# The 24 adaptive sums of layer 0's attention as products on GpSimd and accumulating copies on ScalarE

## The chip, the cores and the metric

One core of a Trainium2 chip runs the whole program. The metric is the device time of one execution in microseconds. The names in the rows are those of the profile: PE is TensorE, PEld its weight loads, DVE is VectorE, ACT is ScalarE, POOL is GpSimd, SP is the engine that issues nearly all transfers.

## What is computed

A two-layer encoder on 512 positions of width 1024. In each layer a vector `c` gives six modulation vectors, three kinds of attention run side by side on groups of heads (differential, dilated windows, two-dimensional neighbourhood), and a gated MLP with a short convolution follows.

```
for l in range(DEPTH):
    mod = jax.nn.silu(c) @ w_ada[l] + b_ada[l]
    sh_a, sc_a, gt_a, sh_f, sc_f, gt_f = [m[:, None, :] for m in jnp.split(mod, 6, axis=-1)]
    h = rms_norm(x, g_attn[l]) * (1.0 + sc_a) + sh_a
    x = x + gt_a * hybrid_mixer(h, w_in[l], ...)
    h = rms_norm(x, g_ffn[l]) * (1.0 + sc_f) + sh_f
    x = x + gt_f * conv_glu_ffn(h, w_up[l], ...)
return rms_norm(x, g_final)
```

The change concerns `mod`: 6144 numbers a layer, each a sum of 1024 products and a bias.

## The kernel before

The activations stand transposed, 128 features on the partitions by 512 positions. Every large product is made on PE as three float32r products (`mm3`, L493 to L495: high times high, high times low, low times high). So each block of weights is loaded as float32 into a buffer of the pool tag `raw` (four buffers; `emit_raw`, L333), ACT casts it to its high part (`whi`, `fhi`, L355), and the rest `raw - whi` is written as the low part in pieces of 256 columns by POOL (L361) or in one piece by DVE (L363), by the kind of weight.

The modulation isn't made on PE. `ada_list` names 96 blocks of 128 outputs, 48 for a layer. For each, `ada_load` (L400 to L410) brings 128 columns of `w_ada` (transposed, 128x1024, 512 KB) into a buffer: the first 16 into buffers of their own, all later ones into the same four `raw` buffers that the weights go through. `ada_step` (L412 to L432) then lets DVE multiply the block with `silu(c)` (`cb`), sum it up along the row and add the bias in one instruction (L422; a second, short one reads the accumulator), which gives one column of `mod`. For the two scale vectors ACT makes `gsc`, `(1 + mod) * g`, from it (L430). Then `ada_step` issues the next load at once, so one block is under way at a time.

The sums run inside other work. `attention_phase` has a list of units (projections, scores, softmax, outputs) and a `Clock`: `ck.after(lag, f)` runs `f` so many ticks later in program order. In layer 0, from the tenth unit on, every fourth tick calls `ada_step` until 40 blocks are done; what is left is done in a loop at the end of the phase (L1216). These are blocks 16 to 39: the gate of the attention, and shift and scale of the FFN. The FFN of layer 0 makes the remaining 56, one every four of its ticks. There are no sums in layer 1.

`ffn_phase` first finishes the output projection (`o2`, four weight units). Each result is added to `x` on DVE (L1223), squared on ACT (L452) and the squares are added up on POOL (L454), first for columns 0 to 255 of all eight blocks, then for the others. PE sums the first half over the partitions (`Norm.stats`, L463), DVE and POOL make the root (L466, L468), and the normed input `h` goes into the gate products (`g0`, `u0`). Order on PE: the first half of `o2`, two blocks of the second half, the statistics of the first half, the rest of the second half, then the gate.

A scheduler orders instructions on each engine, each engine's queue runs in order, and a pool's buffer goes to the next load that asks after it was freed.

Of the kernel before, what the change touches and what calls it, by code (L numbers as in the profile page):

```python
# [14 lines left out]
BF16 = mybir.dt.bfloat16  # L15
AF = mybir.ActivationFunctionType
ALU = mybir.AluOpType
# [4 lines left out]
D = 1024  # L22
# [144 lines left out]
OFF_B = 0  # L167
OFF_GA = OFF_B + NB_ADA
OFF_GF = OFF_GA + DEPTH * 8
# [7 lines left out]
def build(ctx, tc, a):  # L177
    nc = tc.nc
    V, A, G, PE, SY = nc.vector, nc.scalar, nc.gpsimd, nc.tensor, nc.sync
# [14 lines left out]
    def uid():  # L194
        cnt[0] += 1
        return cnt[0]
# [5 lines left out]
    def tmp(shape=(128, 512), dt=F32, tag="tmp", bufs=TMP_BUFS):  # L202
        return wp.tile(list(shape), dt, tag=tag, bufs=bufs, name=f"{tag}{uid()}")

    par = cp.tile([128, NPAR], F32, name="par")
    cb = cp.tile([128, D], F32, name="cb")
# [20 lines left out]
    mod = [cp.tile([128, 48], F32, name=f"mod{l}") for l in range(DEPTH)]  # L227
    gsc = [cp.tile([128, 16], F32, name=f"gsc{l}") for l in range(DEPTH)]
# [83 lines left out]
    ck = Clock()  # L312
# [85 lines left out]
    ada_st = {"n": 0}  # L398

    def ada_load():  # L400
        i = ada_st["n"] + len(ada_raw)
        if i >= len(ada_list):
            return
        l, j = ada_list[i]
        if i < 16:
            r = fpool["p"].tile([128, D], F32, tag="araw", bufs=10, name=f"araw{uid()}")
        else:
            r = wp.tile([128, D], F32, tag="raw", bufs=4, name=f"raw{uid()}")
        SY.dma_start(r, a["w_ada"][l, j])
        ada_raw.append(r)  # L410

    def ada_step():  # L412
        if ada_st["n"] >= len(ada_list):
            return
        if not ada_raw:
            ada_load()
        l, j = ada_list[ada_st["n"]]
        cv = cx if ada_st["n"] < 16 else cb
        r = ada_raw.pop(0)
        ada_st["n"] += 1  # L420
        junk = tmp((128, D), BF16)
        V.tensor_tensor_reduce(out=junk, in0=r, in1=cv, op0=ALU.mult, op1=ALU.add, scale=1.0,  # L422
                               scalar=par[:, OFF_B + l * 48 + j:OFF_B + l * 48 + j + 1],
                               accum_out=mod[l][:, j:j + 1])
        g, k = divmod(j, 8)
        if g in (1, 4):
            o = 0 if g == 1 else 8
            base = OFF_GA if g == 1 else OFF_GF
            g = par[:, base + l * 8 + k:base + l * 8 + k + 1]
            A.activation(out=gsc[l][:, o + k:o + k + 1], in_=mod[l][:, j:j + 1], func=AF.Identity, scale=g, bias=g)  # L430
        if ada_st["n"] >= 16 or ada_st["n"] + len(ada_raw) < 16 and l == 0:
            ada_load()  # L432
# [74 lines left out]
    def first_g0():  # L507
# [47 lines left out]
        with tc.issue_after(last.ins):  # L555
            ada_step()
        ada_step()
        norm_x(0)
        norm_x(1)
        mk(0)  # L560
        norm_x(2)
        norm_x(3)
        ada_step()
        ada_step()
        mk(1)
# [827 lines left out]
    out = a["out"].rearrange("m p n -> p m n")  # L1393
# [62 lines left out]
```

## Time and profile before

| what | value |
|---|---|
| median of 3 runs | 1336.28 us (1334.36 to 1337.09) |
| the profiled execution | 1336.97 us, its span 1335.1 us (1.9 us lie around the span) |
| granted clock of PE, mean | 0.988 |
| busy PE / PEld | 1283.9 / 1100.8 us (96% / 82%) |
| busy DVE | 843.5 us (63%) |
| busy ACT | 632.0 us (47%) |
| busy POOL | 276.3 us (21%) |
| 80 sums on DVE (L422) | 106.9 us, 1336 ns each; idle before them 65.1 us |

The span goes from the first to the last instruction on record. In layer 0 the attention with its projections takes from about 56 to 295 us: differential scores to 143.9 us, the dilated part to 228.8, the neighbourhood part to 295, then the last projection and the norm ahead of the FFN, which begins to multiply at about 319 us. An engine's idle time is put down to what released it.

### The profile page before, as it was taken

What the parts mean: (1) busy time and instruction counts of PE and PEld (TensorE: products, weight loads), DVE (VectorE), ACT (ScalarE), POOL (GpSimd) and SP (SyncE); (2) the same over time, 40 slices, a digit from 0 to 9 for tenths busy, and PEclk for the clock granted to TensorE, in tenths of its full rate; (3) what the DMA queues carried; (4) which work ended last, traced back from release to release, by engine and by line L of the source; (5) the groups of instructions that cost most, each with busy time, mean ns of one, the idle gap of its engine ahead of it and who ended that gap; (6) DMA issues with size and microseconds to landing.
All of it is one profiled execution on the core that took longest, in us unless ns stands there. A gap on an engine that the chain in (4) does not pass through costs nothing.

```text
span 1335.1 us, 18663 instructions
## 1 busy us (share of the span) xinstructions
PE 1283.9 (96%) x6836; PEld 1100.8 (82%) x6836; DVE 843.5 (63%) x1538; ACT 632.0 (47%) x1138; POOL 276.3 (21%) x351
## 2 busy tenths in 40 slices
PE   6989899889999999999999999999999999999997
PEld 5878688779988888888899878988898888888886
DVE  6669777688776566656766596566775434443443
ACT  5446588665533233323342577887553313331331
POOL 4646623243000000000022465323500000000002
PEclk9999999899999999999999999999999999999999
DMA  9776568853465656665523856572343333333211
GB/s 360 253 205 179 173 201 215 237 158 126 147 206 181 203 171 190 193 201 166 175 81 116 205 144 193 145 205 83 115 127 95 95 97 97 95 96 103 77 36 63
DMA packets 75003, 207.30 MB, mean 155 GB/s; under 512 B 8608, under 2 KB 12576, under 8 KB 74784
## 3 DMA queue, kind: packets, MB, share of 16 engines
q1 hardware_dynamic: 74048, 203.72, 50.9%
q10 hardware_dynamic: 864, 2.39, 0.5%
q8 instruction: 54, 0.88, 0.3%
q14 instruction: 37, 0.30, 0.1%
HBM read 180.91 MB, written 15.73 MB: 147 GB/s over the span
## 4 chain that ended last, share of the span: by engine, by line
PE 77%; DMA 10%; DVE 5%; POOL 3%; issue 3%; ACT 2%; SPq 1%; POOLq 0%; DVEq 0%; ACTq 0%
PE pr L495 10%; PE pr L493 10%; PE pr L494 10%; PE s L494 5%; PE s L493 5%; PE s L495 5%; PE pt L494 4%; PE pt L493 4%; PE pt L495 4%; DMA raw<-w 3%; PE pt L923 2%; PE o L494 2%; PE o L495 2%; PE o L493 2%; DMA raw<-w_ada 2%
## 5 line engine op out<-in xcount | busy, mean ns | idle before, releaser
L355 ACT CAST whi<-raw 128x1024 fp32r<-128x1024 f32 (+2 forms) x136 | 128.3, 944 | 240.0 <-PE pr L495 76.9
L454 POOL TENSOR_TENSOR tmp<-tmp,tmp 128x256 f32<-128x256 f32 (+1 forms) x38 | 38.6, 1017 | 708.2 <-ACT tmp L452 707.2
L361 POOL TENSOR_TENSOR wlo<-raw,whi 128x256 fp32r<-128x256 f32 (+1 forms) x170 | 123.8, 759 | 226.0 <-ACT whi L355 201.7
L363 DVE TENSOR_TENSOR wlo<-raw,whi 128x1024 fp32r<-128x1024 f32 (+1 forms) x86 | 100.3, 1167 | 101.8 <-ACT whi L355 101.1
L422 DVE CUSTOM_DVE_ANT_0 tmp<-raw,cb,par 128x1024 bf16<-128x1024 f32 x80 | 106.9, 1336 | 65.1 <-DMA raw<-w_ada 64.8
L355 ACT CAST fhi<-raw 128x1024 fp32r<-128x1024 f32 (+1 forms) x76 | 74.5, 985 | 129.3 <-PE pr L495 51.8
L363 DVE TENSOR_TENSOR flo<-raw,fhi 128x1024 fp32r<-128x1024 f32 (+1 forms) x74 | 86.5, 1169 | 55.5 <-ACT fhi L355 54.7
L493 PE MATMUL pr<-h,whi 128*128 128x512 f32 (+1 forms) x300 | 112.8, 376 | 1.4 <-DVE tmp L677 0.7
L495 PE MATMUL pr<-h,whi 128*128 128x512 f32 (+1 forms) x300 | 111.9, 373 | 0.4 <-DVE h L489 0.4
L494 PE MATMUL pr<-h,wlo 128*128 128x512 f32 (+1 forms) x300 | 112.1, 374 | 0.0
L493 PE MATMUL pr<-h,fhi 128*128 128x512 f32 (+1 forms) x244 | 86.9, 358 | 0.1
L494 PE MATMUL pr<-h,flo 128*128 128x512 f32 (+1 forms) x244 | 86.7, 357 | 0.0
L495 PE MATMUL pr<-h,fhi 128*128 128x512 f32 (+1 forms) x244 | 85.9, 358 | 0.3 <-DVE h L489 0.3
L1281 ACT ACTIVATE tmp<-tmp 128x512 f32<-128x512 f32 x44 | 27.6, 631 | 80.1 <-DVE tmp L1276 80.1
L493 PEld LDWEIGHTS pr<-h,whi 128*128 128x128 f32 x300 | 56.9, 190 | 10.3 <-ACT whi L355 1.0
L495 PEld LDWEIGHTS pr<-h,whi 128*128 128x128 f32 x300 | 56.9, 190 | 9.5 <-DVE h L489 0.6
L494 PEld LDWEIGHTS pr<-h,wlo 128*128 128x128 f32 x300 | 57.0, 190 | 8.5
L931 DVE TENSOR_TENSOR pl<-pt,ph 128x512 fp32r<-128x512 f32 x80 | 54.5, 684 | 14.0 <-ACT ph L927 13.8
L927 ACT CAST ph<-pt 128x512 fp32r<-128x512 f32 x80 | 46.5, 583 | 29.1 <-PE pt L923 28.4
L1017 DVE TENSOR_REDUCE sm<-s 128x1 f32<-128x512 f32 x64 | 43.0, 681 | 21.1 <-PE s L1015 20.7
L1025 ACT ACTIVATE tmp<-s,sm 128x512 f32<-128x512 f32 x64 | 43.8, 690 | 18.9 <-DVE sm L1017 16.5
L493 PE MATMUL pr<-oh,whi 128*128 128x512 f32 (+1 forms) x128 | 49.7, 388 | 3.0 <-ACT oh L1164 3.0
(288 smaller groups left out, 3694.6 us busy)
## 6 DMA issues: line engine op xcount, KB each, us to landing
raw<-w SPq DMA_DIRECT2D x132, 512.0 KB
raw<-w_ada SPq DMA_DIRECT2D x80, 512.0 KB
raw<-w SPq DMA_DIRECT2D x64, 384.0 KB
araw<-w_ada SPq DMA_DIRECT2D x16, 512.0 KB
raw<-w SPq DMA_DIRECT2D x16, 320.0 KB
graw<-w SPq DMA_DIRECT2D x8, 384.0 KB
scr0b<-nat SPq DMA_DIRECT2D x12, 256.0 KB
qs<-nat SPq DMA_DIRECT2D x24, 128.0 KB
```

Of the source, the lines that this page charges most:

```text
L355: A.copy(hi, r)
L361: G.tensor_tensor(out=lo[:, c:e], in0=r[:, c:e], in1=hf[:, c:e], op=ALU.subtract)
L363: V.tensor_tensor(out=lo, in0=r, in1=hi.bitcast(F32), op=ALU.subtract)
L422: V.tensor_tensor_reduce(out=junk, in0=r, in1=cv, op0=ALU.mult, op1=ALU.add, scale=1.0, scalar=par[:, OFF_B + l * 48 + j:OFF_B + l * 48 + ...
L454: self.last = self.eng.tensor_tensor(out=self.sq[0][:, sl], in0=self.sq[0][:, sl], in1=self.sq[m][:, sl], op=ALU.add)
L493: PE.matmul(out, wh, hh, start=first, stop=False)
L494: PE.matmul(out, wl, hh, start=False, stop=False)
L495: return PE.matmul(out, wh, hl, start=False, stop=last)
L927: A.copy(st["ph", half][:, :, sl], pt)
L931: V.tensor_tensor(out=st["pl", half][:, :, sl], in0=st["pt", qb], in1=st["ph", half][:, :, sl].bitcast(F32), op=ALU.subtract)
L1017: V.tensor_reduce(out=nm[:, m:m + 1], in_=s, axis=AX.X, op=ALU.max, negate=True)
L1025: A.activation(out=Ps[m], in_=ss[m], func=AF.Exp, bias=nm[:, m:m + 1], accum_out=dn if m else ld)
```

## The change

For blocks 16 to 39 of layer 0 the instruction on DVE is gone. In its place POOL multiplies the block with `cb` in four pieces of 256 columns, in place in the `raw` buffer. Two ticks later ACT copies the product as bf16 into a scratch tile and accumulates along the row, adds the bias with a second instruction, and makes `gsc` where needed. The load of the next block is issued only there, behind ACT's copy, no longer at once. The 16 blocks ahead and the 56 blocks behind stay as they are. Lines behind L420 have numbers higher by 21.

```diff
--- before.py
+++ after.py
@@ -418,6 +418,27 @@
         cv = cx if ada_st["n"] < 16 else cb
         r = ada_raw.pop(0)
         ada_st["n"] += 1
+        g, k = divmod(j, 8)
+        if l == 0 and 16 <= ada_st["n"] - 1 < 40:
+            for c0 in range(0, D, 256):
+                G.tensor_tensor(out=r[:, c0:c0 + 256], in0=r[:, c0:c0 + 256], in1=cb[:, c0:c0 + 256], op=ALU.mult)
+
+            def fin():
+                junk = tmp((128, D), BF16)
+                acc = tmp((128, 1), tag="sm1", bufs=12)
+                b = par[:, OFF_B + l * 48 + j:OFF_B + l * 48 + j + 1]
+                A.activation(out=junk, in_=r, func=AF.Copy, accum_out=acc)
+                A.activation(out=mod[l][:, j:j + 1], in_=acc, func=AF.Identity, bias=b)
+                if g in (1, 4):
+                    o = 0 if g == 1 else 8
+                    base = OFF_GA if g == 1 else OFF_GF
+                    gp = par[:, base + l * 8 + k:base + l * 8 + k + 1]
+                    A.activation(out=gsc[l][:, o + k:o + k + 1], in_=mod[l][:, j:j + 1], func=AF.Identity,
+                                 scale=gp, bias=gp)
+                ada_load()
+
+            ck.after(2, fin)
+            return
         junk = tmp((128, D), BF16)
         V.tensor_tensor_reduce(out=junk, in0=r, in1=cv, op0=ALU.mult, op1=ALU.add, scale=1.0,
                                scalar=par[:, OFF_B + l * 48 + j:OFF_B + l * 48 + j + 1],
```

The order on POOL in the dilated part, before. `wlo` are the low parts of weights, `sm` a root.

```order
L986 TENSOR_TENSOR sm_1815<-sm_1812,mh 128x8
L361 TENSOR_TENSOR wlo_1878<-raw_1663,whi_1877 128x256 x3
L361 TENSOR_TENSOR wlo_2002<-raw_1774,whi_2001 128x256 x3
L361 TENSOR_TENSOR wlo_2113<-raw_1883,whi_2112 128x256 x3
L361 TENSOR_TENSOR wlo_2205<-raw_2007,whi_2204 128x256 x4
```

The same place after:

```order
L361 TENSOR_TENSOR wlo_1908<-raw_1681,whi_1907 128x256 x3
L424 TENSOR_TENSOR raw_1929<-raw_1929,cb 128x256 x4
L361 TENSOR_TENSOR wlo_2038<-raw_1798,whi_2037 128x256 x3
L424 TENSOR_TENSOR raw_2064<-raw_2064,cb 128x256 x4
L361 TENSOR_TENSOR wlo_2155<-raw_1913,whi_2154 128x256 x3
L424 TENSOR_TENSOR raw_2166<-raw_2166,cb 128x256 x4
```

Between any two splits stands the product of one block, four pieces on the block's own buffer.

POOL at the start of the FFN, before. `flo` is the low part of the last `o2` weight, L454 the additions of the squares.

```order
L361 TENSOR_TENSOR wlo_3271<-raw_3156,whi_3270 128x256 x3
L361 TENSOR_TENSOR wlo_3323<-raw_3219,whi_3322 128x256 x3
L361 TENSOR_TENSOR flo_3372<-raw_3276,fhi_3371 128x256 x3
L454 TENSOR_TENSOR tmp_3402<-tmp_3402,tmp_3415 128x512
L454 TENSOR_TENSOR tmp_3402<-tmp_3402,tmp_3435 128x256
L454 TENSOR_TENSOR tmp_3402<-tmp_3402,tmp_3449 128x256
L454 TENSOR_TENSOR tmp_3402<-tmp_3402,tmp_3463 128x256
L454 TENSOR_TENSOR tmp_3402<-tmp_3402,tmp_3477 128x256
L454 TENSOR_TENSOR tmp_3402<-tmp_3402,tmp_3491 128x256
```

The same place after; L475 is the addition that was L454.

```order
L361 TENSOR_TENSOR wlo_3385<-raw_3258,whi_3384 128x256 x3
L361 TENSOR_TENSOR wlo_3437<-raw_3327,whi_3436 128x256 x3
L424 TENSOR_TENSOR raw_3449<-raw_3449,cb 128x256 x4
L424 TENSOR_TENSOR raw_3478<-raw_3478,cb 128x256 x4
L361 TENSOR_TENSOR flo_3501<-raw_3390,fhi_3500 128x256 x3
L475 TENSOR_TENSOR tmp_3531<-tmp_3531,tmp_3544 128x512
L424 TENSOR_TENSOR raw_3484<-raw_3484,cb 128x256 x4
L475 TENSOR_TENSOR tmp_3531<-tmp_3531,tmp_3564 128x256
L475 TENSOR_TENSOR tmp_3531<-tmp_3531,tmp_3578 128x256
L424 TENSOR_TENSOR raw_3490<-raw_3490,cb 128x256 x4
L475 TENSOR_TENSOR tmp_3531<-tmp_3531,tmp_3592 128x256
L475 TENSOR_TENSOR tmp_3531<-tmp_3531,tmp_3606 128x256
```

Four of the 24 products stand from here on, the last two of them between the additions of the first half's squares.

ACT ahead of the norm, before. `oh` is the high part of the last attention output, `fhi` are weights of `o2` and `u0`, L452 the squares.

```order
L355 CAST whi_3322<-raw_3219 128x768
L957 COPY tmp_3342<-o_3331 64x512
L430 ACTIVATE gsc_100<-mod_98,par 128x1
L1164 CAST oh_3345<-of_3290 128x512
L355 CAST fhi_3371<-raw_3276 128x768
L355 CAST fhi_3379<-raw_3328 128x768
L430 ACTIVATE gsc_100<-mod_98,par 128x1
L452 ACTIVATE tmp_3402<-x_78 128x512
```

The same place after. L430 is now the accumulating copy, L431 the bias, L436 is `gsc`, L473 the squares.

```order
L430 ACTIVATE tmp_3445,sm_3446<-raw_3379 128x1024
L431 ACTIVATE mod_98<-sm_3446,par 128x1
L355 CAST whi_3436<-raw_3327 128x768
L978 COPY tmp_3462<-o_3451 64x512
L1185 CAST oh_3465<-of_3404 128x512
L430 ACTIVATE tmp_3473,sm_3474<-raw_3449 128x1024
L355 CAST fhi_3500<-raw_3390 128x768
L431 ACTIVATE mod_98<-sm_3474,par 128x1
L355 CAST fhi_3508<-raw_3442 128x768
L436 ACTIVATE gsc_100<-mod_98,par 128x1
L473 ACTIVATE tmp_3531<-x_78 128x512
```

The accumulating copies of blocks 35 and 36 have come in between; those of 37 to 39 stand further down, among the `h` of the gate.

The built program gives each load an address. By these, blocks 23, 24, 25, 26, 28, 29, 31 and 36 load into the buffer that ACT's copy of the block just before them frees, and block 38 into that of block 36.

## Rows read from the trace of the kernel before

**Rows 1.** The page, part 4: shares of the chain that ended last, by engine.
```profile
PE 77%; DMA 10%; DVE 5%; POOL 3%; issue 3%; ACT 2%; SPq 1%; POOLq 0%; DVEq 0%; ACTq 0%
```

**Rows 2.** Waits of PE, 56 to 313 us: total us, times, longest.
```profile
PE s L1092 <- issue: 5.1, 1, 5.1
PE s L1050 <- DVE sm L1054: 4.5, 1, 4.5
PE pr L493 <- ACT oh L1164: 2.8, 1, 2.8
PE s L1015 <- DMA qs<-scr0d: 2.1, 1, 2.1
```

**Rows 3.** Waits of DVE, the same stretch.
```profile
DVE tmp L422 <- DMA raw<-w_ada: 17.3, 5, 6.6
```

**Rows 4.** Timeline of DVE, line L422: start, duration, [idle before, releaser].
```profile
163.72 1.28 DVE L422 CUSTOM_DVE_ANT_0 tmp<-raw,cb,par 128x1024 bf16<-128x1024 f32 x1 [5.94 <-DMA raw<-w_ada]
229.18 1.28 DVE L422 CUSTOM_DVE_ANT_0 tmp<-raw,cb,par 128x1024 bf16<-128x1024 f32 x1
291.80 1.28 DVE L422 CUSTOM_DVE_ANT_0 tmp<-raw,cb,par 128x1024 bf16<-128x1024 f32 x1 [2.63 <-DMA raw<-w_ada]
```

**Rows 5.** Timeline of PE: last projection of layer 0 begins; statistics of the FFN norm.
```profile
295.01 0.58 PE L493 MATMUL pr<-oh,whi 128*128 128x512 f32 x1 [2.75 <-ACT oh L1164]
309.52 1.05 PE L463 MATMUL pt<-cst,tmp 128*128 128x1 f32 x8 [1.84 <-POOL tmp L454]
```

**Rows 6.** Timeline of ACT around the three late loads and the norm's squares.
```profile
165.66 0.72 ACT L1059 ACTIVATE tmp<-tmp,sm 128x512 f32<-128x512 f32 x1 [8.00 <-DVE sm L1054]
166.38 1.32 ACT L1064 ACTIVATE tmp<-tmp,sm 128x512 f32<-128x512 f32 x2
247.43 0.40 ACT L1115 ACTIVATE tmp<-tmp,sm 128x128 f32<-128x128 f32 x1 [5.88 <-DVE sm L1106]
293.13 0.39 ACT L430 ACTIVATE gsc<-mod,par 128x1 f32<-128x1 f32 x1 [3.08 <-DVE mod L422]
299.99 0.62 ACT L452 ACTIVATE tmp<-x 128x512 f32<-128x512 f32 x1
```

**Rows 7.** Table by stretches, line L422 alone: stretch, us, DVE busy (count).
```profile
143.90:228.80 84.90, 12.10 (x18) 0.98 0.69 206
```

**Rows 8.** Table by stretches: us, busy PE PEld DVE ACT POOL, clock, DMA, GB/s.
```profile
100.00:143.90 43.90, 43.47 (x231) 35.12 (x230) 41.71 (x80) 28.88 (x64) 29.45 (x36) 0.99 0.62 168
143.90:228.80 84.90, 79.48 (x457) 70.13 (x458) 59.51 (x142) 63.87 (x131) 31.47 (x41) 0.98 0.69 206
228.80:295.00 66.20, 57.07 (x321) 47.66 (x319) 48.98 (x141) 45.85 (x116) 18.92 (x27) 0.95 0.70 196
```

**Rows 9.** Timeline of POOL, one split in three pieces.
```profile
254.30 1.85 POOL L361 TENSOR_TENSOR wlo<-raw,whi 128x256 fp32r<-128x256 f32 x3 [18.62 <-ACT whi L355]
```

**Rows 10.** Instructions of ACT by line and form, 56 to 313 us: busy, mean ns.
```profile
L355 ACT CAST whi<-raw 128x1024 fp32r<-128x1024 f32 x10 | 10.5, 1046 | 1.5 <-POOL tmp L685 1.1 <-PE pr L495 0.3
L1059 ACT ACTIVATION_READ_ACCUMULATOR tmp<-tmp,sm 128x1 f32 x24 | 4.6, 190 | 0.0
L430 ACT ACTIVATE gsc<-mod,par 128x1 f32<-128x1 f32 x8 | 3.1, 386 | 5.6 <-DVE mod L422 5.6
```

**Rows 11.** Timeline of SP's queue, two loads of blocks for the sums.
```profile
157.59 0.54 SPq L409 DMA_DIRECT2D raw<-w_ada  x1
288.12 0.33 SPq L409 DMA_DIRECT2D raw<-w_ada  x1
```

**Rows 12.** Timeline of POOL at the start of the FFN of layer 0.
```profile
297.04 3.21 POOL L361 TENSOR_TENSOR flo<-raw,fhi 128x256 fp32r<-128x256 f32 x3 [5.54 <-ACT fhi L355]
...
306.94 3.21 POOL L454 TENSOR_TENSOR tmp<-tmp,tmp 128x256 f32<-128x256 f32 x3 [0.39 <-ACT tmp L452]
```

**Rows 13.** Instructions of DVE by line and form, 56 to 313 us.
```profile
L1165 DVE TENSOR_TENSOR ol<-of,oh 128x512 fp32r<-128x512 f32 x3 | 3.5, 1176 | 2.0 <-ACT oh L1164 2.0
L896 DVE TENSOR_TENSOR ol<-of,oh 128x512 fp32r<-128x512 f32 x5 | 3.4, 682 | 0.7 <-ACT oh L895 0.7
```

## The prediction

> **What bounds the kernel now.** I read the chain first: TensorE stands for 77% of the chain that ended last, VectorE for 5%, the transfers for 10% [rows 1]. So an edit that lightens VectorE is worth what TensorE waits for VectorE in the stretch that is touched, and no more. That stretch is the attention of layer 0 (56 to 295 us) and the start of its FFN. Its waits of TensorE come next [rows 2]: only three are long, 4.5, 5.1 and 2.8 us. The first names VectorE as releaser, the second nothing, the third a cast on ScalarE. VectorE's own waits say what is behind [rows 3]: it stood 17.3 us in five places, always in front of a sum of `ada_step` whose block hadn't landed. The first gap shows the pattern: VectorE waits 5.94 us until 163.72 us [rows 4], then does what was queued behind, ScalarE gets the score it needs and starts at 165.66 after 8.00 us of idling [rows 6], and TensorE goes on. In the same way the longest wait of VectorE, 6.6 us [rows 3], stands in front of ScalarE's 5.88 us at 247.43 [rows 6] and TensorE's 5.1, and the 2.63 us before 291.80 [rows 4] in front of ScalarE's 3.08 [rows 6] and TensorE's 2.75 at 295.01 [rows 5]. So the sums cost time by late data in a queue, in three gaps with 4.5 + 5.1 + 2.75 = 12.35 us, and not by VectorE's work on them. The table by stretches gives the room of each engine [rows 8]: in the dilated part (143.9 to 228.8 us) VectorE has 59.5 and ScalarE 63.9 of 84.9 us; in the neighbourhood part (228.8 to 295) they have 49.0 and 45.9 of 66.2.
>
> **What goes.** VectorE loses 24 instructions with their reads. In the dilated part these are nine with 12.10 us [rows 7], 1.34 us each, in all 32 us. Its occupancy there falls from 59.5 to 47.4. None of that is TensorE's time beyond the three gaps.
>
> **What comes on GpSimd.** Four products of 128x256 for each sum. The nearest instruction is the split L361 of the same shape: three in 1.85 us where nothing disturbs them [rows 9], three in 3.21 at the FFN start [rows 12]. Four make 2.5 or 4.3 us; I take 3.0, nearer to the attention's row, where most of them run. GpSimd then holds 31.5 + 9 x 3.0 = 58.5 of 84.9 us and 18.9 + 27 = 45.9 of 66.2 us [rows 8]: room enough, but each product puts 3 us between landing and result, and the accumulation still follows, where VectorE took 1.28 for both.
>
> **What comes on ScalarE.** A copy of 128x1024 with accumulation: the cast of the same shape takes 1.05 us, the read of an accumulator 0.19, the small Identity as much as L430's, 0.39 [rows 10]. ScalarE starts an instruction before the last one's recorded end: an activation of 0.72 us and its read of 0.19 begin at 165.66, the next at 166.38 [rows 6], 0.19 less than their sum. So 1.63 us of busy time occupy about 1.4. In the dilated part ScalarE goes to 63.9 + 9 x 1.4 = 76.5 of 84.9 us, in the neighbourhood part to 45.9 + 12.6 = 58.5 of 66.2 [rows 8].
>
> **What the wait turns into.** The loads aren't issued sooner, and the accumulating copy stands in ScalarE's queue only two ticks behind the place of the old sum. If a block lands late, ScalarE now waits for landing plus product. The first gap: landing at 163.7 [rows 4], product done at 166.7, while ScalarE stood free from 165.66 - 8.00 = 157.7 on [rows 6]. That is about 8 us of waiting again, in front of the casts and exponentials that TensorE waits for. So I don't book the 12.35 us as a gain. Dilated part: 76.5 + 8.5 = 85 if all else that ScalarE idles there now (84.9 - 63.9 - 8.0 = 13) is absorbed, 98 if none of it is: 0 to +13 us. It idles there mostly while TensorE is busy, since TensorE's other waits are 2.1 us or less [rows 2], so I stay near the lower end, **+3**. Neighbourhood part: 58.5 + 9 (5.88 + 3.08) = 67.5 against 66.2, plus at most 66.2 - 45.9 - 9 = 11.3 of other idling: +1 to +13, I take **+3**. Below both: if the product is always done when ScalarE gets there, the gaps go, -4.5 and -7.85. Ahead of 143.9 us VectorE is busy 41.7 of 43.9 us [rows 8] and gains three times 1.34; ScalarE and GpSimd have 15.0 and 14.5 us of room, of which the three sums take 4.2 and 9: **0**.
>
> **The start of the FFN** is where I see a cost without an offset. TensorE reaches the last projection at 295.01 [rows 5], the squares start on ScalarE at 299.99 [rows 6], and TensorE waits for GpSimd's additions already, 1.84 us at 309.52 [rows 5]. In the new order (printed above) the products of the last two sums stand between these additions, and the accumulation of sum 36 in front of the cast of the last `o2` weight and of all squares. Sum 36 loads into the buffer that the accumulation of sum 35 frees, and sum 38 into the one that 36 frees. A turn of that loop is issue 0.3 to 0.5, transfer, product 3.0, accumulation 1.2. The transfer took 291.80 - 288.12 = 3.7 us in one place and 163.72 - 157.59 = 6.1 in another [rows 4, 11]; I take 4, as the first stands here. Count from the projection's start. The accumulation of 35 ends about 1 us before (it stands three instructions in front of the last `oh`), that of 36 comes 8.6 later, at 7.6, so the squares begin 2.6 us later than the 5 us of now. Sum 38's product can begin at 7.6 + 0.45 + 4 = 12 and end at 15; two additions (1.07 each, three in 3.21 [rows 12]) and the product of 39 carry this to 20, four more additions to 24.4. Now the additions are through at 306.94 + 3.21 = 310.15 [rows 12], 15.1 us after the projection's start. That is 9 us late; some additions may stand elsewhere than I count them, so **+8**. Its ends are 2.5 (one product of 2.5 us, all else beside the squares) and 11 (both transfers at about 5 to 6 us). TensorE's queue is in order behind these statistics, so nothing covers it.
>
> **Sum.** 0 + 3 + 3 + 8 = +14 us on the profiled execution's 1336.97 us, which stands 0.7 us above the median of 1336.28: **1351 us**. Lower bound -4.5 - 7.85 + 2.5 = -9.9, 1327 us. Upper 13 + 13 + 11 = +37, 1374 us, though all three at their ends together I hold for unlikely.
>
> One rule speaks against the change. A split of 128x512 on VectorE takes 1176 ns on average at L1165 and 682 at L896 [rows 13], so half a us is lost there to something. The Trainium skill ("SBUF — State Buffer", on the port pair that VectorE and GpSimd share) says that a VectorE instruction with two SBUF inputs and a GpSimd instruction that reads SBUF exclude each other, each for the other's whole duration. By it 96 more GpSimd pieces would meet such instructions more often; if only these eight splits met one, VectorE would lose an estimated 4 us of its 32 and my sum would stay as it is.
>
> **Rivals.**
> - *Relief wins.* The products run at 2.5 us and are ready when ScalarE comes, VectorE isn't held any more: the three gaps go (-12.35), the FFN start costs 2.5 to 9. For it: VectorE stood in front of all three gaps [rows 3, 4]. Against: landing, not VectorE, was late. 1327 to 1334 us. Chance 0.22.
> - *It evens out.* Half of the gaps go, -6, the FFN start costs 4 to 8: 1334.3 to 1339.6 us. Chance 0.13.
> - *The loop through one raw buffer sets the pace.* The next load is issued only after the accumulation, and eight of the loads up to sum 36 take just the buffer that this frees (four dilated, four behind). A turn is 1.2 + 0.45 + 3.7 to 6.1 + 2.5 to 4.3 = 7.9 to 12 us; the sums stand (229.18 - 163.72) / 8 = 8.2 us apart in the dilated part and (291.80 - 229.18) / 8 = 7.8 behind [rows 4]. Where a turn is longer, ScalarE stands still for the difference: at 10 us 4 x 1.8 + 4 x 2.2 = 16, at 12 us 32, with the FFN start +24 to +40, less some that other idling absorbs: 1361 to 1376 us. It decides from turns of 9 us on. Chance 0.18.
> - *VectorE is slowed by GpSimd's pieces* as in the paragraph on rows 13: 96 pieces x 0.5 = 48 us against the 32 that it gains, so no relief and later results for ScalarE, +18 to +28: 1355 to 1365. Chance 0.03.
> - That the change doesn't do what it says is out: the products stand on GpSimd in the order printed above.
>
> **How the numbers follow.** My forecast, 1340 to 1361, has 0.44. A measurement of this kernel can tell about 0.2%, 2.7 us, from no change: faster 0.22, same 0.13, slower 0.44 + 0.18 + 0.03 = 0.65. The range from 1329 to 1370 leaves out the lowest part of the first rival (0.06), the upper part of the third (0.08) and a little on both sides for what I haven't seen.
>
> **What would show it.** Right: in the new trace ScalarE waits at L430 for L424, 10 us and more in all, ahead of TensorE's gaps; VectorE's waits at L422 in layer 0's attention are gone; from the projection's start to the statistics of the first half there are 21 to 25 us in place of 14.5, with TensorE waiting for an addition of L475. Wrong: ScalarE finds the products done (waits below 3 us in all), or the statistics come no later. If the third rival holds, the waits at L430 are regular, 2 to 5 us each, in most of the sums.

## The result

The changed kernel takes 1381.76 us (median of 4 runs, 1379.27 to 1383.82) against 1336.11 us (4 runs, 1334.36 to 1337.09): ratio 1.0336, 95% interval 1.0316 to 1.0356. It is 45 us slower, outside the range of 1329 to 1370; the side was right, the size was a third of what came. The profiled execution took 1380.75 us with a span of 1379.0, 43.9 us more than before.

The page of the changed kernel, parts 1 and 4 (busy us and share by engine; shares of the chain that ended last):

```profile
PE 1297.5 (94%) x6836; PEld 1110.7 (81%) x6836; DVE 813.3 (59%) x1490; ACT 661.2 (48%) x1210; POOL 339.8 (25%) x447
...
PE 72%; DMA 9%; POOL 7%; ACT 4%; issue 4%; DVE 3%; SPq 0%; POOLq 0%; DVEq 0%; ACTq 0%
```

The work moved as counted: VectorE has 30.2 us less, ScalarE 29.2 and GpSimd 63.5 us more (843.5, 632.0 and 276.3 before). In the chain GpSimd and ScalarE went from 3% and 2% to 7% and 4%, and VectorE from 5% to 3% [rows 1]. TensorE is busy 13.6 us longer with the same 6836 matmuls, so they took longer on average.

The waits of ScalarE, GpSimd and TensorE from 56 to 375 us (total us, times, longest):

```profile
ACT tmp L430 <- POOL raw L424: 51.5, 16, 8.5
...
POOL raw L424 <- DMA raw<-w_ada: 39.6, 12, 10.3
...
PE pt L1018 <- ACT tmp L1012: 8.2, 1, 8.2
PE o L965 <- ACT ph L948: 8.0, 3, 6.6
PE pt L484 <- POOL tmp L475: 7.5, 1, 7.5
PE o L1168 <- DVE of L981: 5.5, 2, 2.8
PE pt L1151 <- ACT tmp L1142: 4.6, 2, 4.2
```

These answer [rows 2, 3]. VectorE's 17.3 us in front of late blocks are gone; in their place ScalarE waits 51.5 us for products, in 16 of 24 sums, and GpSimd 39.6 us for blocks. Where TensorE had four gaps of 1 us or more between 100 and 310 us (14.2 us; the three of [rows 2] and the 1.84 us of [rows 5]), it has thirteen between 100 and 352 us (44.3 us), eight of them behind ScalarE.

The table by stretches of the changed kernel, cut at the same places of the program as [rows 8] (first dilated score, first neighbourhood score, last projection, statistics of the second half; columns as there):

```profile
100.00:155.50 55.50, 45.63 (x237) 37.30 (x235) 38.04 (x75) 31.93 (x72) 35.41 (x46) 0.94 0.55 158
155.50:245.60 90.10, 80.90 (x447) 69.53 (x448) 45.65 (x116) 71.93 (x153) 53.19 (x75) 0.96 0.60 172
245.60:330.50 84.90, 64.43 (x320) 54.04 (x318) 41.71 (x128) 58.29 (x145) 40.65 (x59) 0.84 0.53 147
330.50:363.70 33.20, 24.63 (x154) 22.94 (x154) 15.00 (x28) 13.49 (x27) 23.81 (x31) 0.79 0.31 97
```

The last of these stretches in the kernel before:

```profile
295.00:319.00 24.00, 21.30 (x154) 19.97 (x155) 20.31 (x35) 13.01 (x25) 14.79 (x16) 0.93 0.57 178
```

The dilated part starts 11.6 us late (155.5 for 143.9 us) and takes 5.2 us more (90.1 for 84.9). The neighbourhood part takes 18.7 us more (84.9 for 66.2), at a granted clock of 0.84 where it was 0.95. From the last projection to the statistics of the first half it is 21.5 us, 7.0 more than the 14.5 before. These four make 42.5 of the 43.9 us. A mean clock of 0.84 is a mixture of two levels, 2.4 GHz (1.00) and 1.2 GHz (0.50): from 253.0 to 266.6 us it stands at 0.50, around a gap of TensorE of 6.64 us that ends at 261.94; in the 8 us ahead of that TensorE was busy for 6.0 at 1.00.

**The first jam.** The product of block 17 on GpSimd, the copy on ScalarE and TensorE around it, in the changed kernel's timelines (start, duration, [idle before, releaser]):

```profile
123.14 1.65 POOL L1007 TENSOR_TENSOR sm<-sm,mh 128x8 f32<-128x8 f32 x1
...
132.82 2.76 POOL L361 TENSOR_TENSOR wlo<-raw,whi 128x256 fp32r<-128x256 f32 x4
135.54 2.77 POOL L424 TENSOR_TENSOR raw<-raw,cb 128x256 f32<-128x256 f32 x4
147.54 3.28 POOL L361 TENSOR_TENSOR wlo<-raw,whi 128x256 fp32r<-128x256 f32 x4 [9.23 <-ACT whi L355]
150.78 2.83 POOL L424 TENSOR_TENSOR raw<-raw,cb 128x256 f32<-128x256 f32 x4
```

```profile
138.34 1.06 ACT L430 ACTIVATE tmp<-raw 128x1024 bf16<-128x1024 f32 x1 [8.51 <-POOL raw L424]
...
139.40 0.60 ACT L1012 COPY tmp<-sm 128x512 f32<-128x512 f32 x1
...
146.41 1.05 ACT L355 CAST whi<-raw 128x1024 fp32r<-128x1024 f32 x1 [0.68 <-PE pr L516]
...
153.64 1.06 ACT L430 ACTIVATE tmp<-raw 128x1024 bf16<-128x1024 f32 x1 [5.69 <-POOL raw L424]
```

```profile
140.05 2.08 PE L1018 MATMUL pt<-cst,tmp 128*128 128x128 f32 x8 [8.22 <-ACT tmp L1012]
```

Read from the top: GpSimd works almost without a pause from 123.14 to 138.3 us on a root, rotary products and splits, and the product of block 17 is the last of it. The data are not late there (the product has no idle time in front of it). ScalarE stands still for 8.51 us until it is done, and behind the accumulating copy in ScalarE's queue is the copy L1012 that TensorE waits for, 8.22 us. Then it turns round: the next split on GpSimd waits 9.23 us for the cast of 146.41, which ScalarE reached late, and the product of block 18 stands behind that split; ScalarE waits 5.69 us for it. Two queues that each run in order wait for each other by turns.

**The late load.** The same views at the start of the neighbourhood part:

```profile
240.21 2.86 SPq L906 DMA_DIRECT2D va<-scv  x4
243.17 0.43 SPq L409 DMA_DIRECT2D raw<-w_ada  x1
```

```profile
255.80 2.76 POOL L424 TENSOR_TENSOR raw<-raw,cb 128x256 f32<-128x256 f32 x4 [10.28 <-DMA raw<-w_ada]
```

```profile
258.60 1.06 ACT L430 ACTIVATE tmp<-raw 128x1024 bf16<-128x1024 f32 x1 [8.25 <-POOL raw L424]
```

```profile
261.94 1.22 PE L965 MATMUL o<-ph,vb 128*128 128x256 f32 x4 [6.64 <-ACT ph L948]
```

The copy of one block ends at 242.3 us and frees the buffer of the next. SP's queue issues four transfers of 384 KB until 243.07, and the load right behind them, at 243.17. Issue to product is 12.6 us. GpSimd waits 10.28, ScalarE 8.25, TensorE 6.64 us: one late block is handed through three queues and little of it gets lost on the way.

What the loads wait for in SP's queue says how the ring closes. Before (56 to 313 us):

```profile
SPq L409 <- POOL wlo L361: 21.2, 10, 3.3
```

After (56 to 375 us):

```profile
SPq L409 <- POOL wlo L361: 46.0, 13, 7.6
...
SPq L409 <- ACT tmp L430: 17.0, 5, 4.4
```

ScalarE's copy itself is the last thing that a load waits for in five places, 17.0 us. In thirteen places, 46.0 us, it is a weight split on GpSimd that still reads a buffer, and the splits now stand between the products in GpSimd's queue. (Most of the rest, 21.1 us in nine places, is ScalarE's casts of weights.) A late product thus makes a late split, this a late load, and this the next late product.

**The norm.** GpSimd at the start of the FFN, answering [rows 12], and TensorE's statistics, answering [rows 5]:

```profile
340.65 1.28 POOL L475 TENSOR_TENSOR tmp<-tmp,tmp 128x512 f32<-128x512 f32 x1
341.90 2.81 POOL L424 TENSOR_TENSOR raw<-raw,cb 128x256 f32<-128x256 f32 x4
344.67 1.52 POOL L475 TENSOR_TENSOR tmp<-tmp,tmp 128x256 f32<-128x256 f32 x2
346.16 3.48 POOL L424 TENSOR_TENSOR raw<-raw,cb 128x256 f32<-128x256 f32 x4
349.60 3.00 POOL L475 TENSOR_TENSOR tmp<-tmp,tmp 128x256 f32<-128x256 f32 x4
```

```profile
351.98 1.86 PE L484 MATMUL pt<-cst,tmp 128*128 128x1 f32 x8 [7.55 <-POOL tmp L475]
```

Two products of 2.8 and 3.5 us lie between the additions, and TensorE waits 7.55 us where it waited 1.84.

### The profile page after: what moved, and what is told of

Same layout as the page of the kernel before. It is cut to its first block, busy times and chain, and to the rows that moved or that the text cites. A ratio compares the mean times of both kernels' runs of the same rounds, so it can differ in the third digit from the quotient of the medians.

```text
span 1379.0 us, 18801 instructions
## 1 busy us (share of the span) xinstructions
PE 1297.5 (94%) x6836; PEld 1110.7 (81%) x6836; DVE 813.3 (59%) x1490; ACT 661.2 (48%) x1210; POOL 339.8 (25%) x447
## 4 chain that ended last, share of the span: by engine, by line
PE 72%; DMA 9%; POOL 7%; ACT 4%; issue 4%; DVE 3%; SPq 0%; POOLq 0%; DVEq 0%; ACTq 0%
PE pr L516 10%; PE pr L514 10%; PE pr L515 9%; PE s L515 5%; PE s L514 5%; PE s L516 5%; PE pt L515 4%; PE pt L514 4%; PE pt L516 4%; DMA raw<-w_ada 4%; POOL raw L424 3%; POOL wlo L361 2%; PE o L514 2%; PE o L515 2%; PE o L516 2%
## 5 line engine op out<-in xcount | busy, mean ns | idle before, releaser
L475 POOL TENSOR_TENSOR tmp<-tmp,tmp 128x256 f32<-128x256 f32 (+1 forms) x38 | 36.6, 966 | 707.2 <-ACT tmp L473 706.5
L363 DVE TENSOR_TENSOR flo<-raw,fhi 128x1024 fp32r<-128x1024 f32 (+1 forms) x74 | 86.9, 1176 | 73.7 <-ACT fhi L355 73.1
L443 DVE CUSTOM_DVE_ANT_0 tmp<-raw,cb,par 128x1024 bf16<-128x1024 f32 x56 | 71.6, 1278 | 13.8 <-DMA raw<-w_ada 13.7
L424 POOL TENSOR_TENSOR raw<-raw,cb 128x256 f32<-128x256 f32 x96 | 69.2, 754 | 39.6 <-DMA raw<-w_ada 39.6
L514 PEld LDWEIGHTS pr<-h,whi 128*128 128x128 f32 x300 | 57.4, 191 | 11.3 <-DVE tmp L698 1.4
L944 PE MATMUL pt<-cst,tmp 128*128 128x128 f32 x320 | 50.5, 282 | 8.3 <-DVE pl L952 3.4
L1244 DVE SCALAR_TENSOR_TENSOR x<-pr,mod,x 128x512 f32<-128x512 f32 (+1 forms) x40 | 24.8, 627 | 56.0 <-PE pr L516 55.7
L1038 DVE TENSOR_REDUCE sm<-s 128x1 f32<-128x512 f32 x64 | 42.9, 681 | 21.1 <-PE s L1036 20.4
```

Source lines behind the costliest of these rows:

```text
L363: V.tensor_tensor(out=lo, in0=r, in1=hi.bitcast(F32), op=ALU.subtract)
L424: G.tensor_tensor(out=r[:, c0:c0 + 256], in0=r[:, c0:c0 + 256], in1=cb[:, c0:c0 + 256], op=ALU.mult)
L514: PE.matmul(out, wh, hh, start=first, stop=False)
L944: PE.transpose(pt[:, kt], P[:, kt * 128:kt * 128 + 128], ident)
L1038: V.tensor_reduce(out=nm[:, m:m + 1], in_=s, axis=AX.X, op=ALU.max, negate=True)
```

## The experiments

Two theories stood at first. **A**: the data come late, since the next load is issued only behind ScalarE's copy. **B**: the data aside, the accumulating copy stands too early in ScalarE's queue, in front of work that TensorE needs, and waits for a GpSimd that is busy or itself waiting. A third, the extra work by itself, was to be ruled out. Here is what all runs gave; a point below is 0.01 of the ratio. The positions are the first dilated score, the first neighbourhood score, the first residual of the last projection and the first statistics, in us of the profiled execution; the ratio is to the kernel before on the same chip.

| run | ratio (95%) | dilated | neighb. | residual | statistics |
|---|---|---|---|---|---|
| before | 1 | 143.9 | 228.8 | 297.3 | 309.5 |
| changed | 1.0336 (1.0316 to 1.0356) | 155.5 | 245.6 | 332.5 | 352.0 |
| early load | 1.0153 (1.0116 to 1.0190) | 150.8 | 236.3 | 314.1 | 328.8 |
| six ticks | 1.0226 (1.0197 to 1.0255) | 142.8 | 225.7 | 307.7 | 333.0 |
| early load, six ticks | 1.0096 (1.0063 to 1.0128) | 141.5 | 225.8 | 296.2 | 320.8 |
| the same, last five on VectorE | 1.0064 (1.0039 to 1.0090) | 141.4 | 225.2 | 303.0 | 316.0 |
| no product | 1.0039 (1.0020 to 1.0058) | 142.2 | 233.2 | 306.3 | 318.7 |
| work alone, both | 1.0092 (1.0058 to 1.0126) | 142.7 | 229.5 | 301.6 | 319.7 |
| work alone, GpSimd | 1.0102 (1.0087 to 1.0117) | 143.9 | 234.0 | 304.8 | 322.1 |
| work alone, ScalarE | 1.0026 (1.0007 to 1.0044) | 143.6 | 231.2 | 299.9 | 313.2 |
| first three on VectorE | 1.0265 (1.0241 to 1.0290) | 143.7 | 237.7 | 322.7 | 342.5 |
| last four on VectorE | 1.0304 (1.0272 to 1.0336) | 154.0 | 246.0 | 338.7 | 351.7 |
| before, sum four ticks later | 0.9951 (0.9937 to 0.9966) | 141.5 | 221.8 | 286.7 | 301.2 |
| before, sum six ticks later | 1.0020 (1.0008 to 1.0033) | 142.7 | 230.1 | 296.4 | 311.9 |

**Early load.**

```diff
+            ada_load()
             ck.after(2, fin)
...
-                ada_load()
```

> One edit to the changed kernel: the next block's load is issued again right behind the products, in ada_step, and no longer behind ScalarE's accumulating copy. Theory A (the late issue and the loop through one buffer make the data late): GpSimd's waits for blocks fall from 39.6 to under 15 us, ScalarE's waits at the accumulating copy from 51.5 to under 20, and the time to 1345 to 1358. Theory B (the two in-order queues hold each other up: ScalarE's copy waits for a product that stands behind splits or other work on GpSimd, which in turn wait for ScalarE): GpSimd's waits for blocks fall too, but ScalarE's stay at 35 us or more and the time at 1368 to 1380.

1357.47 us: 1.83 points of 3.36 come back, a time at the upper end of what theory A gave. But the waits say that it isn't the whole. ScalarE's and GpSimd's waits in this run (56 to 380 us):

```profile
ACT tmp L430 <- POOL raw L424: 29.4, 9, 6.2
...
POOL raw L424 <- DMA raw<-w_ada: 31.1, 9, 7.4
```

ScalarE still waits 29.4 us, more than A's 20 and less than B's 35, and GpSimd waits 31.1, where A expected less than 15: neither theory has the waits right. A load issued at the old place still stands behind the attention's own transfers in SP's queue, and still waits for GpSimd's splits, 27.9 us in nine places. The dilated part is still 6.9 us late.

**Early load and six ticks; six ticks alone.**

```diff
-            ck.after(2, fin)
+            ck.after(6, fin)
```

> As the run with the early load, and ScalarE's copy stands six ticks behind the products in place of two. Theory A expects about what the early load alone gives, 1345 to 1358. Theory B expects ScalarE's waits at the copy to fall below 8 us, whatever GpSimd does, and 1335 to 1346; what then stays over the kernel before is ScalarE's and GpSimd's extra work and the start of the FFN.

> The changed kernel with ScalarE's copy six ticks behind the products in place of two, the load still behind the copy. With early load and two ticks the time was 1357, with both 1349. If the late issue alone is the cause (theory A), this is worse than or equal to the changed kernel, since the loads are issued four ticks later still: 1380 to 1400, with GpSimd and not ScalarE waiting longest for blocks. If ScalarE's place in its queue is the cause (theory B), 1350 to 1365.

Both together: 1348.99 us. The time lies in A's range and not in B's 1335 to 1346, and it is 8.5 us less than with the early load alone, where A expected about the same. Six ticks alone: 1363.08 us, inside B's 1350 to 1365 and far from A's 1380 or more. But this run is weaker evidence than its expectation takes it for, since the loads aren't four ticks later in it. `ada_step` runs every four ticks. At two ticks the copy of one block issues the load of the next, two ticks ahead of its product. At six ticks the copy stands behind the next block's product and issues the load of the block after that, again two ticks ahead of its product; only the load of block 17 comes directly before its own. So what the run changes is the copy's place and, with it, the ring, which now goes over two blocks instead of one; the lateness of the load stays the same. A's sign in the waits came even so: GpSimd waits 53.2 us for blocks (39.6 in the changed kernel), ScalarE 35.9 at the copies.

The copy's place is worth 1.10 points with the load behind the copy (1.0336 to 1.0226) and 0.57 with the early one, the latter hardly clear of the intervals. Both are net: the residual comes 24.8 and 17.9 us sooner, but the stretch from residual to statistics grows, from 19.5 to 25.3 and from 14.7 to 24.5 us. The load's place is worth 1.83 points at two ticks and 1.30 at six. Together they make 2.40 of 3.36 points, 32 us, and the attention is then no later than before (residual at 296.2 for 297.3 us). The waits of that run and TensorE's longest:

```profile
ACT tmp L430 <- POOL raw L424: 27.2, 11, 9.0
...
POOL raw L424 <- DMA raw<-w_ada: 51.8, 12, 13.9
...
PE pt L484 <- POOL tmp L475: 11.3, 1, 11.3
```

ScalarE's waits did not fall below 8 us as B expected; they cost TensorE less where they now stand. The statistics come 11.3 us later than before, and that is what is left over the kernel before; TensorE's gap in front of them is 11.3 us too.

**No product.** The four GpSimd instructions of each block are left out:

```diff
-            for c0 in range(0, D, 256):
-                G.tensor_tensor(out=r[:, c0:c0 + 256], in0=r[:, c0:c0 + 256], in1=cb[:, c0:c0 + 256], op=ALU.mult)
```

> The changed kernel without GpSimd's products: ScalarE sums up the raw block two ticks later, so the modulation of layer 0's attention gate and FFN is left wrong, and the load is still issued behind that copy. Theory A: the transfers stay late, ScalarE waits for them itself, 30 us or more at the copies, 1360 to 1375. Theory B: without products ScalarE waits under 20 us there and the time is 1340 to 1352.

Here ScalarE sums up the blocks as they were loaded. 1343.90 us, a time in B's range. ScalarE's wait in front of its copies, directly for the block:

```profile
ACT tmp L428 <- DMA raw<-w_ada: 23.9, 5, 9.3
```

That is 23.9 us in five places for 51.5 in 16; B expected less than 20, A 30 or more. With the load issued at the same late place, behind the copy, only 0.39 points are left. Two things go with the product: its 2.8 us in GpSimd's queue, and the early need for the block. The first to ask for it is now the copy, four ticks behind the load as in the kernel before, and no longer a product two ticks behind it. The run doesn't tell these two apart. What it shows is that the place of the load is expensive only together with the product: A and B are not two causes side by side but two halves of one loop.

**The work alone.** To the kernel before, with its sums on VectorE, is added (both, and each by itself):

```diff
+        if l == 0 and 16 <= ada_st["n"] - 1 < 40:
+            pj = tmp((128, 256))
+            for c0 in range(0, D, 256):
+                G.tensor_tensor(out=pj, in0=cb[:, c0:c0 + 256], in1=cb[:, c0:c0 + 256], op=ALU.mult)
+            def extra():
+                aj = tmp((128, D), BF16)
+                acc = tmp((128, 1), tag="sm1", bufs=12)
+                A.activation(out=aj, in_=cb, func=AF.Copy, accum_out=acc)
+                A.activation(out=acc, in_=acc, func=AF.Identity)
+            ck.after(2, extra)
```

> The kernel before, sums on VectorE and loads as they were, plus the new work alone and without its waits: 24 times four 128x256 products on GpSimd and, two ticks later, an accumulating copy of 128x1024 and a small Identity on ScalarE, all on a resident tile. Theories A and B both say that the work by itself is hidden: 1336 to 1343. A third theory (ScalarE, 64 of 85 us busy in the dilated part, has no room for 1.4 us a sum; or GpSimd's pieces slow VectorE down) gives 1348 to 1362.

> The kernel before plus GpSimd's four pieces a block on a resident tile alone, without ScalarE's copies. Both kinds of work together cost 12 us, of which 6 lie between the first residual and the statistics. If GpSimd's pieces between the norm's additions make these 6 and more, this run gives 1344 to 1350 and the stretch is again 17 us or longer; if it is ScalarE, 1336 to 1340 and 12 to 13 us.

> The kernel before plus ScalarE's copies on a resident tile alone, without GpSimd's pieces. The complement: if GpSimd makes the cost, 1336 to 1340; if ScalarE's room is what counts, 1343 to 1350.

Both together 1349.74 us, so the work is not hidden, against theories A and B. GpSimd's part alone gives 1348.16, ScalarE's alone 1338.99: nearly all of it is GpSimd's. GpSimd's timeline of its own run, at the end of the attention:

```profile
299.42 9.88 POOL L424 TENSOR_TENSOR tmp<-cb 128x256 f32<-128x256 f32 x11
309.26 1.71 POOL L361 TENSOR_TENSOR flo<-raw,fhi 128x256 fp32r<-128x256 f32 x1
310.92 0.61 POOL L424 TENSOR_TENSOR tmp<-cb 128x256 f32<-128x256 f32 x1
311.50 1.41 POOL L361 TENSOR_TENSOR flo<-raw,fhi 128x256 fp32r<-128x256 f32 x2
312.87 2.69 POOL L424 TENSOR_TENSOR tmp<-cb 128x256 f32<-128x256 f32 x4
315.51 7.23 POOL L458 TENSOR_TENSOR tmp<-tmp,tmp 128x512 f32<-128x512 f32 x7
```

The last blocks' pieces come in a heap, since the loop at the phase's end calls `ada_step` for all that is left; 9.88 us of them stand in front of the low part `flo` of the last weight, 2.69 in front of the norm's additions. From residual to statistics it is 17.3 us, as expected of GpSimd (12.2 before, 13.3 in ScalarE's run). 7.5 us were lost before, in the attention; part of that belongs to the experiment, since VectorE had to wait 6.7 us once for a scratch tile that these pieces held, which the changed kernel doesn't do. So the third theory holds in its amount, 0.92 points for both kinds of work, and with the ring mended at both places 0.96 points were left. That the two numbers are alike fits, but the time isn't lost at the same places (residual at 301.6 us here, 296.2 there).

**First three, last four and last five blocks on VectorE.**

```diff
-        if l == 0 and 16 <= ada_st["n"] - 1 < 40:
+        if l == 0 and 19 <= ada_st["n"] - 1 < 40:
```

> The changed kernel, with only the first three blocks (16 to 18, in the differential part) on VectorE as before. There GpSimd's product of block 17 stood behind 12 us of other work and ScalarE waited 8.5 and 5.7 us. If that is what made the dilated part start 11.6 us late, it now starts within 2 us of the kernel before and the time is 1368 to 1374. If the lateness is made up further on, 1377 or more.

1371.58 us. The dilated part starts at 143.7 us, as in the kernel before (143.9), and some 10 of the 11.6 us arrive at the end. The jam around blocks 17 and 18 is a term that can be taken away by itself.

For the last four the bound 40 becomes 36 in the changed kernel; for the last five 35, with early load and six ticks.

> The changed kernel, with only the last four blocks (36 to 39) on VectorE as before, so no product stands among the norm's additions. If these products are what delays the statistics, the stretch from the first residual to the statistics returns from 19.5 us (12.2 in the kernel before) to 12 to 14, the loop at the attention's end loses its last turns too, and the time falls by 8 to 14 us, to 1367 to 1374. If ScalarE's late squares alone delay them, less than 3 us come back.

> Early load and copy six ticks later as in the run before, and the last five blocks (35 to 39) on VectorE. With the early load and six ticks the first residual came at 296.2 us (297.3 in the kernel before) but the statistics 11.3 us later than before. If GpSimd's products among the additions are the whole of that, the statistics come within 2 us of the kernel before and the time is 1334 to 1340; if the extra work in the attention costs too, 1341 to 1348.

The last four: 1379.14 us, less than the 8 to 14 expected; by the ratios, whose intervals overlap (1.0304 and 1.0336), not surely anything. The stretch from residual to statistics did return to 13.0 us, from 19.5. But the residual came 6.2 us later (338.7 for 332.5, in the slowest of the four executions, 1383.33 us). Some of this is VectorE's doing, which now waits for a late block ahead of the last projection's low part:

```profile
335.20 1.29 DVE L443 CUSTOM_DVE_ANT_0 tmp<-raw,cb,par 128x1024 bf16<-128x1024 f32 x1 [3.11 <-DMA raw<-w_ada]
```

It waits 3.11 us and then makes two sums of 1.3 us in front of the residual at 338.71. In this place the delay was moved, not removed. With the ring mended the last five on VectorE give 1345.74 us, inside the second alternative's 1341 to 1348, and it is the same again: the stretch returns to 13.0 us from 24.5, the residual comes 6.8 us later, and the statistics come 4.8 us sooner than with all on GpSimd, but still 6.5 us later than before.

**Before, with the sum deferred.** No work moves between engines. VectorE's sum, put into a function `fin`, runs four, or six, ticks later, and the next load stays where it was (without the lines of `fin`):

```diff
+        if l == 0 and 16 <= ada_st["n"] - 1 < 40:
+            ada_load()
+            ck.after(4, fin)
+            return
```

> The kernel before with VectorE's sum, unchanged, four ticks behind its old place, while the next load is still issued at the old place, for the same 24 blocks. Theory A+B (the data's lateness in an in-order queue is what costs, on whatever engine): VectorE's 17.3 us of waiting fall below 6, the three gaps of TensorE shrink, and the time is 1324 to 1333. If VectorE's work is the cost, nothing moves: 1335 to 1340.

> The kernel before with VectorE's sum six ticks behind its old place, the load where it was. At four ticks VectorE still waited 13.1 us for blocks in seven places and the time was 1331.7 against 1338.3 in the same runs. If the waits are only moved further out by more ticks, 1326 to 1331; if the rest of them comes from transfers that share the engines with the attention's own, the same 1329 to 1334; the buffers held longer may cost the weights something, 1334 or more.

Four ticks: 1331.68 us against 1338.31 us of the kernel before on the same chip, ratio 0.9951: faster than both kernels. VectorE's waits for blocks, and TensorE's longest, in that run:

```profile
DVE tmp L423 <- DMA raw<-w_ada: 13.1, 7, 5.8
...
PE pr L502 <- DVE ol L903: 4.6, 1, 4.6
PE pt L470 <- POOL tmp L461: 2.0, 1, 2.0
```

The waits of VectorE fell only from 17.3 to 13.1 us, not below 6. But of TensorE's three gaps [rows 2, 5] two are gone, 4.5 and 2.75 us. The 4.6 us are what is left of the middle one, at the same place of the neighbourhood part and behind the same kind of wait:

```profile
239.13 1.28 DVE L423 CUSTOM_DVE_ANT_0 tmp<-raw,cb,par 128x1024 bf16<-128x1024 f32 x1 [5.75 <-DMA raw<-w_ada]
```

The low part `ol` stands right behind this sum, and TensorE goes on with it at 241.09 us. The residual comes 10.6 us sooner. The two gaps make 7.25 us and the run is 6.6 us faster, which fits the price that the prediction put on late data in VectorE's queue.

Six ticks: 1338.76 us, no gain, slightly slower than before. VectorE waits less (6.5 us), but from the first dilated to the first neighbourhood score it takes 87.4 us for 80.3 at four ticks, and then TensorE waits 4.5 us for a transfer `qs<-nat`. In program order up to three of the four `raw` buffers then belong to blocks, at four ticks two. That this is the reason was only argued; no run separates it.

## Why the prediction was wrong

**The side and the mechanism.** That the 12.35 us of gaps would not be a gain, because a wait for late data moves from VectorE to ScalarE with the product's time added, was right; the sum deferred by four ticks confirms the gaps as the cost of late data. All the signs named for "right" came: ScalarE waits at L430 for L424 (51.5 us), VectorE's waits at L422 are gone, 21.5 us from projection to statistics, TensorE waiting for L475. They couldn't tell +14 from +45 us.

**What goes and what comes.** VectorE lost 30.2 us (32 forecast), a product took four pieces of 0.74 us, 2.8 us (3.0 forecast). ScalarE's rise of 29.2 us is 1.2 a sum, under the 1.4. The error isn't here. The fourth rival, VectorE slowed by 48 us, is out: its busy time fell by 30.2 of 32 us, so all that it still does took some 2 us more. The pair of lines that the prediction took for a sign of it measured 1233 and 686 ns, for the 1176 and 682 of [rows 13]:

```profile
L1186 DVE TENSOR_TENSOR ol<-of,oh 128x512 fp32r<-128x512 f32 x3 | 3.7, 1233 | 2.5 <-ACT oh L1185 2.5
L917 DVE TENSOR_TENSOR ol<-of,oh 128x512 fp32r<-128x512 f32 x5 | 3.3, 686 | 1.0 <-ACT oh L916 1.0
```

And most of the half microsecond between the two lines isn't GpSimd's. In the kernel before one of the three splits of L1165 ran while GpSimd stood idle (5.54 us until 297.04 [rows 12]), and it took 1.11 us, 0.43 more than the mean at L896:

```profile
294.99 1.11 DVE L1165 TENSOR_TENSOR ol<-of,oh 128x512 fp32r<-128x512 f32 x1 [1.17 <-ACT oh L1164]
```

**The differential part, booked at 0, cost 11.6 us.** This is the first step that failed. It weighed room against work by totals ("ScalarE and GpSimd have 15.0 and 14.5 us of room"). GpSimd's room was there, but its work came in one piece of 15 us and the product stood at the end of it. GpSimd's queue was never read against the place of the copy in ScalarE's: ScalarE stood still for 8.51 us in front of block 17's product and 5.69 in front of block 18's. The run with three blocks on VectorE takes some 10 us of this term away by itself.

**The dilated part, booked at +3, cost 5.2**; within its bounds.

**The neighbourhood part, booked at +3 with +13 as its end, cost 18.7 us.** This is the second step that failed. The bound kept ScalarE's waits for late blocks at their old 9 us (5.88 + 3.08); measured are 20.7 us at L430 from 245.6 to 330.5 us. The blocks come later than before, because the load is issued behind the copy and into a buffer that a delayed split frees late, and one that misses its place lands behind the attention's own transfers: 12.6 us from issue to product in the case shown, where [rows 4, 11] had 3.7 and 6.1.

The third rival named this loop, at 0.18, and came nearest. Its turns of 9 us and more were there: from block 19 to 27 the copies stand 9.6 us apart on average, from 28 to 35 again 9.6, where the sums stood 8.2 and 7.8 apart. It priced turns of 10 us at 16 us in both parts together; they cost 23.9. It counted idling of ScalarE alone, and left out GpSimd's queue: by the runs without products (0.39 points left) and with the early load (1.83 points back) neither the place of the load nor the products alone make up the loss.

**The clock was left out.** TensorE's busy time rose by 13.6 us for the same matmuls, with a granted clock of 0.84 in the neighbourhood part (0.95 before [rows 8]) and 0.79 behind it. Of the 43.9 us nearly a third is this, a term that the sum puts at nothing without a reason. No run holds the clock fixed; that the 13.6 us are the clock's is read from the stretches, where the busy time grows most in those with the lower clock (57.07 to 64.43 us in the neighbourhood part). The kernels with fewer gaps show it from the other side: early load with six ticks has 1282.9 us of TensorE, the deferred sum 1282.3, the kernel before 1283.9.

**The start of the FFN, booked at +8, cost 7.0 us** (14.5 to 21.5), and by the two products between the additions as forecast. Counted from the projection's start the product of sum 38 begins at 11.4 us (12 forecast) and the additions are through at 22.1 (24.4 forecast). As an independent term it was wrong all the same: with the last four sums back on VectorE it returned 6.5 us and 6.2 were lost ahead of it.

**The upper end** of 1370 fell not because the three terms with a range met at their ends: the dilated part and the FFN stayed within theirs. It fell because one of them passed its end, the neighbourhood part (18.7 for 13), and because the differential part, with no range at all, cost 11.6. That the dilated part came out within its bounds is in part luck: ScalarE waited 11.9 us at L430 there, in seven places, where the sum had counted some 8 us in one.

## What to carry to other kernels

Moving a step from one engine to two turned one wait in an order into a ring of queues here. Before such a move is priced, lay the two queues side by side and see what stands in front of the producer and what behind the consumer, instead of comparing free time by totals. Keep a load's issue where its buffer allows it, not behind the last step of the chain that uses the one before. Where an engine waits for late data at the head of its queue, first try to move the waiting instruction down by a few places; here that beat moving the work (0.9951 against 1.0336), and a few places more lost the gain again (1.0020).

## What was not expected of the hardware

GpSimd's pieces kept their time beside all else that ran: of the 92 recorded from 100 to 380 us half took 736 ns or less (717 the shortest, 1437 the longest), and the splits of the same shape stayed at a median of 740 ns for 741. What was lost stands in the order of the queues, not in longer pieces. And the gaps of TensorE went with a second cost: some 30 us of idle time, and 13.6 us more of busy time in the stretches with the lower granted clock.
